# A hybrid decoder block: order of the first projections, of x's sums and of GLA's rstd product

## The chip, the cores and the metric

The kernel runs on one core of one Trainium2 chip. The metric is the device time of one execution in microseconds, the median of the runs shown; less is better.

## The reference, cut to what matters

One layer, batch 1, 256 tokens, model width 1024, all float32. `n = RMSNorm(x)` goes through one combined projection, whose columns are MoBA's q, k, v (512 each), GLA's q, k (512 each), GLA's v (1024), a rank-16 gate, an output gate (1024) and two branch gates (1024 each). MoBA (8 heads of 64) is causal attention with normed q and k and a T5 bias table; GLA (4 heads of 128) is a chunked gated linear attention. Both are mixed, projected, and a squared-ReLU feed-forward block follows.

```python
n = rms_norm(h, norm1_g[layer])
proj = n @ w_in[layer]
(mq, mk, mv, gq, gk, gv, g_low, g_out, gate_moba, gate_gla) = jnp.split(proj, IN_SPLIT_POINTS, axis=-1)
mq = rms_norm(mq.reshape(B, S, MOBA_HEADS, MOBA_HEAD_DIM), moba_q_norm_g[layer])
mk = rms_norm(mk.reshape(B, S, MOBA_HEADS, MOBA_HEAD_DIM), moba_k_norm_g[layer])
y_moba = moba_attention(mq, mk, mv, t5_bias)
log_a = log_sigmoid(g_low @ gla_gate_up + gla_gate_bias) / GLA_GATE_TAU
y_gla = gla_attention(gq, gk, gv, log_a)
h = h + (sigmoid(gate_moba) * (y_moba @ w_branch_moba) + sigmoid(gate_gla) * (norm(y_gla) * silu(g_out) @ w_branch_gla)) @ w_out
h = h + square(relu(rms_norm(h) @ w_up)) @ w_down
```

## The kernel before, in words

Every float32 product is made of three matmuls on parts: each operand is split into a rounded high part and the rest, and high x high, high x low and low x high are added in PSUM. The weights come in units of 1 MB (128 x 4 x 512). SyncE loads a unit (`load`, line 85), ScalarE copies it into the high part `wh` in two halves (`split`, line 94), and VectorE subtracts for the low part `wl` (`rest`, line 98). `rest` also asks for the load of the unit four places on.

The projection runs over `IN_ORDER`: MQ, MK, GQ, GK, MV, GV0, GV1 and so on, two units for each name (`hu` 0 to 25), and each unit in two turns t, one for each 128 tokens, or for GQ and GK one for each 128 columns. A turn is called a slot here: slot = 2 * hu + t. In slot s TensorE gets the unit's matmuls; then `flush` issues what the slot before deferred (its `rest`, and the VectorE part of its evictions); then `split` prepares a half of the unit two places on; then come the eviction of a finished accumulator and the steps that were hung on this slot with `at(slot, ...)`. MQ is slots 0 to 3, MK slots 4 to 7; before the change GQ is slots 8 to 11, GK 12 to 15, MV 16 to 19. Each engine takes its own instructions strictly in this order, so a late one holds all behind it.

Because x goes into the projection without its norm, each eviction multiplies by rstd. `x_stats` (line 237) sums x squared on ScalarE, VectorE and GpSimd make rstd from it (`rsqrt`, lines 218 and 219). MQ and MK are evicted by `m_evac` (lines 301 and 303 on ScalarE, then a reduction, line 308, and a `rsqrt` for each head), at slots 5 to 8 behind the other steps; `m_norm` (316) scales, `m_transpose` (324, then 287 and 288) turns q and k into high and low parts, and `m_scores0` (334) multiplies them, `m_scores1` follows. GQ and GK come out transposed, so their rstd lies along the free axis: `g_diag` and `g_row` (468 to 479) spread it into the row `rrow`, and `g_evac` adds two halves (542 on ScalarE, 545 on VectorE) and multiplies by that row (546 on VectorE). The GLA gate is `g_low` and `g_decay` (488 to 509), in which ScalarE and VectorE take turns on a bank (508, 509).

The T5 bias is made on the chip: `make_bias` (270, 272) puts a small table into DRAM as `ud`, `spread_bias` copies it to 128 rows `ur`, and `load_bias` reads it with a skew into `bias`, which line 345 of `m_scores0` adds. All three DMAs are issued by SyncE, in its queue between the weight loads. SyncE also loads, in this order at the start: x and the MQ weights, units 2 and 3, `vec`, x again for the sums (`xs`), the bias inputs, the gate weights, units 4 and 5.

Of the kernel before, what the change touches and what calls it, by code (L numbers as in the profile page):

```python
# [15 lines left out]
AF = mybir.ActivationFunctionType  # L16
OP = mybir.AluOpType
AX = mybir.AxisListType

S = 256  # L20
D = 1024
NT = 2
H = 8
DH = 64
GH = 4
DK = 128
# [9 lines left out]
MQ, MK, MV, GQ, GK, GV0, GV1 = 0, 512, 1024, 1536, 2048, 2560, 3072  # L36
GLOW = 3584
GO0, GO1, GA0, GA1, GG0, GG1 = 3600, 4112, 4624, 5136, 5648, 6160
TRANSPOSED = (GQ, GK)
IN_ORDER = (MQ, MK, GQ, GK, MV, GV0, GV1, GO0, GO1, GA0, GG0, GA1, GG1)  # L40


V_G2, V_GB, V_OG, V_QG, V_KG, NVEC = 0, 8, 12, 14, 15, 16
# [3 lines left out]
def block_kernel(ctx, tc, xw0_d, xw_d, x_d, vec_d, w_d, up_d, bias_d, out_d):  # L47
    nc = tc.nc
    P = 128
# [11 lines left out]
    def big(name, dt=F32):  # L61
        return t4.tile([P, 1024], dt, name=name, tag="t4")

    def mid(name):
        return t2.tile([P, 512], F32, name=name, tag="t2")
# [7 lines left out]
    def axbank(name):  # L73
        return ps.tile([P, 512], F32, name=name, tag="ax")
# [4 lines left out]
    def load(i, pieces=1):  # L79
        if i >= NHU:  # L80
            return
        raw[i] = wp.tile([P, 4, 512], F32, name=f"raw{i}", tag="raw", bufs=4)
        n = 4 // pieces
        for a in range(0, 4, n):
            nc.sync.dma_start(raw[i][:, a:a + n, :], w_d[i - 2, :, a:a + n, :])

    def split(i, a, n=2):
        if i >= NHU:
            return
        if a == 0:  # L90
            wH[i] = wp.tile([P, 4, 512], F32R, name=f"wh{i}", tag="wh")
            wL[i] = wp.tile([P, 4, 512], F32R, name=f"wl{i}", tag="wl")
        s = slice(a, a + n)
        nc.scalar.activation(wH[i][:, s, :], raw[i][:, s, :], AF.Copy)  # L94
        defer(rest, i, s)
# [10 lines left out]
    def defer(f, *a):  # L106
        deferred.append((f, a))

    def flush():
        now, deferred[:] = list(deferred), []  # L110
        for f, a in now:
            f(*a)
# [26 lines left out]
    vec = const.tile([P, NVEC + 128], F32, name="vec")  # L139
# [10 lines left out]
        nc.sync.dma_start(xw[kt], xw_d[kt - 1])  # L150
    load(2, 2)
    load(3)
    nc.sync.dma_start(vec, vec_d)

    NBR = bias_d.shape[0]
    smallR, smallS = big("smallR"), big("smallS", F32R)
# [66 lines left out]
    xs = [big(f"xs{t}") for t in range(NT)]  # L223
    for t in range(NT):
        nc.sync.dma_start(xs[t], x_d[:, t, :])
    nc.sync.dma_start(biasR, bias_d)
    nc.sync.dma_start(gup, up_d)
    load(4)
    load(5)

    rstd = const.tile([P, NT], F32, name="rstd")
# [14 lines left out]
    T = {}  # L246
# [15 lines left out]
    bias = t4.tile([P, H, 256], F32, name="bias", tag="t8", bufs=3)  # L262
# [5 lines left out]
    def make_bias():  # L268
        pb = axbank("pbias")
        nc.tensor.matmul(pb[:H, :384], biasS[:, :H], biasS[:, H:], start=True, stop=True)  # L270
        u = mid("u")[:H, :384]
        nc.vector.tensor_copy(u, pb[:H, :384])
        T["ud"] = dr.tile([H, 384], F32, name="ud")
        nc.sync.dma_start(T["ud"], u)

    def spread_bias():

        T["ur"] = dr.tile([P, H, 384], F32, name="ur")
        nc.sync.dma_start(T["ur"], T["ud"][None].to_broadcast([P, H, 384]))

    def load_bias():
        ur = T["ur"]
        nc.sync.dma_start(bias, bass.AP(tensor=ur.tensor, offset=ur.offset + 127,
                                        ap=[[H * 384 - 1, P], [384, H], [1, 256]]))

    def split_evac(dH, dL, src, scale):
# [5 lines left out]
    def m_evac(which, t, acc):  # L292
        if which == "mv":
            if t == 0:
                T["mvH"], T["mvL"] = (big(f"mv{a}", F32R).rearrange("p (t c) -> p t c", t=2) for a in "HL")
            split_evac(T["mvH"][:, t, :], T["mvL"][:, t, :], acc, rstd[:, t:t + 1])
            return
        if t == 0:
            T[which] = big(which)
        dst = T[which].rearrange("p (t c) -> p t c", t=2)[:, t, :]  # L300
        nc.scalar.activation(dst, acc, AF.Copy, scale=rstd[:, t:t + 1])
        sq = mid("sq")
        nc.scalar.activation(sq, acc, AF.Square, scale=rstd[:, t:t + 1])
        r = T[which, "r", t] = small("rsm", H)

        def finish():
            ss = small("ssm", H)
            nc.vector.tensor_reduce(ss, sq.rearrange("p (h d) -> p h d", d=DH), axis=AX.X, op=OP.add)
            rsqrt(r, ss, DH)

        defer(finish)
# [160 lines left out]
    rrow = const.tile([P, S], F32, name="rrow")  # L472
# [63 lines left out]
    def g_evac(which, h, acc):  # L536

        if h == 0:
            T[which] = big(which)
        v = T[which][:, h * S:(h + 1) * S]  # L540
        half = mid("half")[:, :S]
        nc.scalar.activation(half, acc[:, S:], AF.Copy)

        def finish():
            nc.vector.tensor_tensor(v, acc[:, :S], half, op=OP.add)
            nc.vector.scalar_tensor_tensor(v, v, DK ** -0.5 if which == "gq" else 1.0, rrow,
                                           op0=OP.mult, op1=OP.mult)

        defer(finish)

# [103 lines left out]
    def gate_evac(which, n, t, acc):  # L654
        if t == 0:
            T[which, n] = big(f"{which}{n}").rearrange("p (t c) -> p t c", t=2)
        nc.scalar.activation(T[which, n][:, t, :], acc, AF.Sigmoid, scale=rstd[:, t:t + 1])

    def gv_evac(g, t, acc):
        if t == 0:  # L660
            for a in "HL":
                T["gv" + a, g] = big(f"gv{a}{g}", F32R).rearrange("p (t c) -> p t c", t=2)
        split_evac(T["gvH", g][:, t, :], T["gvL", g][:, t, :], acc, rstd[:, t:t + 1])

    evac = {
        MQ: lambda t, a: m_evac("mq", t, a), MK: lambda t, a: m_evac("mk", t, a),
        MV: lambda t, a: m_evac("mv", t, a),
        GQ: lambda t, a: g_evac("gq", t, a), GK: lambda t, a: g_evac("gk", t, a),
        GV0: lambda t, a: gv_evac(0, t, a), GV1: lambda t, a: gv_evac(1, t, a),
        GO0: lambda t, a: silu_evac(0, t, a), GO1: lambda t, a: silu_evac(1, t, a),  # L670
        GA0: lambda t, a: gate_evac("A", 0, t, a), GA1: lambda t, a: gate_evac("A", 1, t, a),
        GG0: lambda t, a: gate_evac("G", 0, t, a), GG1: lambda t, a: gate_evac("G", 1, t, a),
    }


    steps = {}

    def at(slot, f, *a):
        steps.setdefault(slot, []).append((f, a))

    at(5, split_bias)
    at(8, make_bias)
    at(4, x_stats)
    at(6, g_diag)
    at(7, low_split)
    at(8, g_row)
    at(9, gup_split)
    at(9, m_norm, "mq", 0)
    at(10, m_norm, "mq", 1)
    at(10, spread_bias)  # L690
    at(11, m_norm, "mk", 0)
    at(11, g_low)
    at(12, m_norm, "mk", 1)
    at(13, m_transpose, "mq", 0)
    at(13, m_transpose, "mq", 1)
    at(14, g_decay, 0)
    at(14, g_decay, 1)
    at(14, load_bias)
    at(15, m_transpose, "mk", 0)
    at(15, m_transpose, "mk", 1)  # L700
    at(16, m_scores0)
    at(16, m_max, 0)
    at(17, m_softmax, 0, 0, 4)
    at(18, m_softmax, 0, 4, 8)
    at(19, m_scores1, 0)
    at(19, m_max, 1)
    at(19, m_weights, 0)
    at(20, m_softmax, 1, 0, 2)
    at(21, m_softmax, 1, 2, 4)
    at(22, m_scores1, 1)  # L710
    at(22, m_max, 2)
    at(22, m_weights, 1)
    at(23, m_softmax, 2, 0, 2)
    at(24, m_softmax, 2, 2, 4)
    at(25, g_logsig)
    at(26, g_scan)
    at(26, m_weights, 2)
    at(27, g_exp, "eb")
    at(28, g_exp, "einv")
    at(29, g_exp, "edec")  # L720
# [24 lines left out]
    at(50, g_yT, 1, 1)  # L745


    hu = 0
    for u, col in enumerate(IN_ORDER):
        acc = [] if col in TRANSPOSED else [(axbank if u == 1 else mmbank)(f"acc{t}") for t in range(NT)]  # L750
        for g in range(2):
            if u == 0:
                for k in range(4):
                    first_block(4 * g + k, acc)
            for t in range(NT):
                if col in TRANSPOSED:
                    acc = mmbank("acct")
                    for k in range(2):
                        block_t(hu, t, k, xHL[k], acc)
                elif u:  # L760
                    block(hu, t, xH[g], xL[g], acc[t], g == 0, g == 1)
                flush()
                split(hu + 2, 2 * t)
                if g == 1 and u < 2:
                    at(5 + 2 * u + t, evac[col], t, acc[t])
                elif col in TRANSPOSED:
                    evac[col](2 * g + t, acc)
                elif g == 1:
                    evac[col](t, acc[t])
                for f, a in steps.pop(2 * hu + t, []):  # L770
                    f(*a)
            hu += 1
    assert not steps


    mxH = [kview(big(f"mxH{g}", F32R)) for g in range(2)]
# [58 lines left out]
    for n in range(2):  # L835
        acc = [mmbank(f"po{t}") for t in range(NT)]
# [77 lines left out]
    acc = [axbank(f"pu{j}") for j in range(4)]  # L914
# [15 lines left out]
    for c in range(1, NC):  # L930
        for b in range(2):
            for j in range(2):
                acc = axbank(f"pu{j}")
# [86 lines left out]
```

## Time and profile before

| what | us |
|---|---|
| median of 3 runs (lowest to highest) | 424.98 (424.61 to 425.13) |
| the profiled execution, its own time | 424.48 |
| its span, first to last instruction | 422.8 |
| TensorE busy | 412.9 (98%) |
| VectorE busy | 285.9 (68%) |
| ScalarE busy | 222.5 (53%) |
| GpSimd busy | 17.8 (4%) |

The profile shows one execution. A busy share is an average over the whole span; a timeline row gives start and length of one instruction, and in brackets how long its engine was idle just before it and what ended that. The end of a matmul is modelled, and neighbours overlap in the rows, so TensorE's pace is read from one start to the next.

### The profile page before, as it was taken

To read this page: it belongs to the slowest core of one execution; us is meant where nothing else is said; L and a number is where in the kernel's file an instruction comes from. 1 tells how busy PE (TensorE), PEld (TensorE's weight loads), DVE (VectorE), ACT (ScalarE), POOL (GpSimd) and SP (SyncE) were. 2 spreads that over 40 slices of the span, in tenths; PEclk is the share of its full clock that TensorE was granted. 3 is DMA by queue.
4 is the path that set the end of the run, shared out by engine and by line. 5 is a ranking of instruction groups with operands and counts; after the bars stand their busy time and mean duration, and the time that the engine had idled before them with its cause. 6 is when DMAs were issued, how large, how long until landed. Compare 5 with 4: busy or idle time off the path is not lost.

```text
span 422.8 us, 5266 instructions
## 1 busy us (share of the span) xinstructions
PE 412.9 (98%) x2072; PEld 345.5 (82%) x2072; DVE 285.9 (68%) x374; ACT 222.5 (53%) x344; POOL 17.8 (4%) x21
## 2 busy tenths in 40 slices
PE   8999979999999999999999999999999999999996
PEld 5877957888888888888888888888888888888885
DVE  5838987688798543874856878848393848474753
ACT  5669562869865464553423446646362726263520
POOL 2006100000002011000000000000000000000000
PEclk9999996999999999999999999999999999999999
DMA  8995783245544252372675445645455463627002
GB/s 281 381 372 203 258 289 122 87 189 200 198 164 156 86 194 99 135 279 84 219 279 188 136 174 198 228 172 212 186 184 214 147 250 112 287 101 298 0 2 99
DMA packets 13848, 78.91 MB, mean 187 GB/s; under 512 B 1448, under 2 KB 3104, under 8 KB 5376
## 3 DMA queue, kind: packets, MB, share of 16 engines
q1 hardware_dynamic: 13392, 77.28, 50.0%
q10 hardware_dynamic: 432, 1.31, 0.9%
q8 instruction: 16, 0.26, 0.2%
q14 instruction: 8, 0.07, 0.0%
HBM read 77.52 MB, written 2.63 MB: 190 GB/s over the span
## 4 chain that ended last, share of the span: by engine, by line
PE 84%; DMA 5%; DVE 5%; ACT 4%; issue 1%; SPq 0%; ACTq 0%
PE pu L131 14%; PE acc L118 8%; PE acc L119 8%; PE acc L120 8%; PE pu L133 7%; PE fa L119 7%; PE fa L120 7%; PE fa L118 7%; DMA raw<-w 4%; PE po L118 2%; PE po L120 2%; PE pg L118 2%; PE po L119 2%; PE pg L120 2%; PE pg L119 2%; DVE wl L98 2%
## 5 line engine op out<-in xcount | busy, mean ns | idle before, releaser
L98 DVE TENSOR_TENSOR wl<-raw,wh 128x1024 fp32r<-128x1024 f32 x132 | 158.2, 1220 | 18.9 <-ACT wh L94 18.7
L94 ACT ACTIVATE wh<-raw 128x1024 fp32r<-128x1024 f32 x132 | 135.2, 1051 | 24.4 <-PE pg L120 9.8
L131 PE MATMUL pu<-hHL,wh 128*128 128x512 f32 x256 | 69.9, 394 | 0.0
L118 PE MATMUL acc<-wh,xHL 128*128 128x512 f32 x160 | 64.6, 404 | 0.0
L119 PE MATMUL acc<-wl,xHL 128*128 128x512 f32 x160 | 63.0, 394 | 0.0
L120 PE MATMUL acc<-wh,xHL 128*128 128x512 f32 x160 | 62.9, 393 | 0.0
L131 PEld LDWEIGHTS pu<-hHL,wh 128*128 128x128 f32 x256 | 44.3, 189 | 6.3
L120 PE MATMUL fa<-wh,fL 128*128 128x512 f32 x124 | 48.4, 390 | 0.0
L119 PE MATMUL fa<-wl,fH 128*128 128x512 f32 x124 | 48.4, 390 | 0.0
L118 PE MATMUL fa<-wh,fH 128*128 128x512 f32 x124 | 48.3, 389 | 0.0
L133 PEld LDWEIGHTS pu<-hHL,wl 128*128 128x128 f32 x256 | 39.3, 189 | 5.4
L133 PE MATMUL pu<-hHL,wl 128*128 128x256 f32 x256 | 40.7, 281 | 0.0
L870 ACT ACTIVATE half<-pu 128x256 f32<-128x256 f32 x32 | 12.0, 377 | 54.4 <-PE pu L133 54.4
L871 DVE TENSOR_TENSOR sq<-pu,half 128x256 f32<-128x256 f32 x32 | 13.5, 423 | 34.9 <-ACT half L870 34.2
L120 PEld LDWEIGHTS acc<-wh,xHL 128*128 128x128 f32 x160 | 30.4, 190 | 6.7
L118 PEld LDWEIGHTS acc<-wh,xHL 128*128 128x128 f32 x160 | 30.5, 190 | 6.3
L119 PEld LDWEIGHTS acc<-wl,xHL 128*128 128x128 f32 x160 | 30.6, 191 | 5.7
L120 PEld LDWEIGHTS fa<-wh,fL 128*128 128x128 f32 x124 | 23.3, 188 | 4.9
L118 PEld LDWEIGHTS fa<-wh,fH 128*128 128x128 f32 x124 | 23.3, 188 | 4.7
L119 PEld LDWEIGHTS fa<-wl,fH 128*128 128x128 f32 x124 | 23.3, 188 | 4.7
L876 ACT ACTIVATE fH<-sq 128x512 fp32r<-128x512 f32 x16 | 10.1, 632 | 20.6 <-DVE sq L873 20.6
L131 PE MATMUL acct<-xHL,wh 128*128 128x512 f32 x64 | 17.6, 396 | 0.0
(232 smaller groups left out, 533.8 us busy)
## 6 DMA issues: line engine op xcount, KB each, us to landing
raw<-w SPq DMA_DIRECT2D x65, 1024.0 KB, 4.8
xw<-xw SPq DMA_DIRECT2D x7, 384.0 KB, 6.5
ur<-ud SPq DMA_DIRECT2D x1, 1536.0 KB, 9.2
raw<-w SPq DMA_DIRECT2D x2, 512.0 KB, 7.3
xs<-xs SPq DMA_DIRECT2D x2, 512.0 KB, 8.7
bias<-ur SPq DMA_DIRECT2D x1, 1024.0 KB, 7.4
xr<-xs ACTq DMA_DIRECT2D x2, 512.0 KB, 4.8
out<-o SPq DMA_DIRECT2D x3, 256.0 KB, 2.0
```

The source lines that it names most:

```text
L94: nc.scalar.activation(wH[i][:, s, :], raw[i][:, s, :], AF.Copy)
L98: nc.vector.tensor_tensor(wL[i][:, s, :], raw[i][:, s, :], wH[i][:, s, :].bitcast(F32), op=OP.subtract)
L118: nc.tensor.matmul(acc, aH[:, k, tk], h, start=start and k == 0, stop=False)
L119: nc.tensor.matmul(acc, aH[:, k, tk], low, start=False, stop=False)
L120: nc.tensor.matmul(acc, aL[:, k, tk], h, start=False, stop=stop and k == 3)
L131: nc.tensor.matmul(acc, tile_(wH, k), a[:, k, :], start=g == 0 and k == 0, stop=False)
L133: nc.tensor.matmul(acc[:, :S], tile_(wL, k), a[:, k, :S], start=False, stop=g == 1 and k == 3)
L870: nc.scalar.activation(half, acc[:, S:], AF.Copy)
L871: nc.vector.tensor_tensor(o, acc[:, :S], half, op=OP.add)
L876: nc.scalar.activation(H, v, AF.Copy)
```

## The change

It moves MV from the fifth place of the projection to the third, so that MV is slots 8 to 11, GQ 12 to 15 and GK 16 to 19. The sums of x go to slot 3 (from 4); MQ's evictions go to slots 4 and 5 (from 5 and 6), MK's stay in slots 7 and 8, and all four are issued ahead of the slot's `split`. Unit 4's load is issued ahead of `vec` and the bias and gate inputs. The three DMAs of the bias are issued by GpSimd, the last at slot 12 (from 14). MoBA's scores, softmax and weights move one slot later each, up to `m_weights` 2, which goes from 26 to 27. In `g_evac` the add takes the scale along in one VectorE instruction, and the product with `rrow` is GpSimd's.

```diff
-IN_ORDER = (MQ, MK, GQ, GK, MV, GV0, GV1, GO0, GO1, GA0, GG0, GA1, GG1)
+IN_ORDER = (MQ, MK, MV, GQ, GK, GV0, GV1, GO0, GO1, GA0, GG0, GA1, GG1)
...
     load(3)
-    nc.sync.dma_start(vec, vec_d)
...
         nc.sync.dma_start(xs[t], x_d[:, t, :])
+    load(4)
+    nc.sync.dma_start(vec, vec_d)
     nc.sync.dma_start(biasR, bias_d)
     nc.sync.dma_start(gup, up_d)
-    load(4)
     load(5)
...
-        nc.sync.dma_start(T["ud"], u)
+        nc.gpsimd.dma_start(T["ud"], u)
...
-        nc.sync.dma_start(T["ur"], T["ud"][None].to_broadcast([P, H, 384]))
+        nc.gpsimd.dma_start(T["ur"], T["ud"][None].to_broadcast([P, H, 384]))
...
-        nc.sync.dma_start(bias, bass.AP(tensor=ur.tensor, offset=ur.offset + 127,
+        nc.gpsimd.dma_start(bias, bass.AP(tensor=ur.tensor, offset=ur.offset + 127,
...
-        nc.scalar.activation(half, acc[:, S:], AF.Copy)
+        scale = DK ** -0.5 if which == "gq" else 1.0
+        nc.scalar.activation(half, acc[:, S:], AF.Copy, scale=scale)
         def finish():
-            nc.vector.tensor_tensor(v, acc[:, :S], half, op=OP.add)
-            nc.vector.scalar_tensor_tensor(v, v, DK ** -0.5 if which == "gq" else 1.0, rrow,
-                                           op0=OP.mult, op1=OP.mult)
+            nc.vector.scalar_tensor_tensor(v, acc[:, :S], scale, half, op0=OP.mult, op1=OP.add)
+            nc.gpsimd.tensor_tensor(v, v, rrow, op=OP.mult)
...
-    at(5, split_bias)
-    at(8, make_bias)
-    at(4, x_stats)
+    at(3, x_stats)
     at(6, g_diag)
-    at(7, low_split)
     at(8, g_row)
+    at(7, split_bias)
+    at(8, low_split)
     at(9, gup_split)
+    at(9, make_bias)
...
+    at(12, load_bias)
...
-    at(14, load_bias)
...
-    at(16, m_scores0)
-    at(16, m_max, 0)
-    at(17, m_softmax, 0, 0, 4)
+    at(17, m_scores0)
+    at(17, m_max, 0)
+    at(18, m_softmax, 0, 0, 4)
...
-    at(26, m_weights, 2)
+    at(27, m_weights, 2)
...
                 flush()
+                for f, a in early.pop(2 * hu + t, []):
+                    f(*a)
                 split(hu + 2, 2 * t)
                 if g == 1 and u < 2:
-                    at(5 + 2 * u + t, evac[col], t, acc[t])
+                    early.setdefault(4 + 3 * u + t, []).append((evac[col], (t, acc[t])))
```

## Rows read from the trace of the kernel before

**Rows 1.** Waits of TensorE: waiter, releaser, total us, times, longest.

```profile
PE ps L334 <- DVE mkL L288: 2.9, 1, 2.9
```

**Rows 2.** Busy time of each engine by stretch, with granted clock and DMA share.

```profile
27.75:33.38 5.63, 4.19 (x21) 2.82 (x20) 3.42 (x9) 5.07 (x10) 2.20 (x2) 1.00 0.77 292
33.38:57.45 24.07, 24.04 (x149) 21.18 (x149) 22.61 (x41) 15.55 (x30) 6.91 (x4) 1.00 0.70 245
57.45:67.15 9.70, 6.08 (x40) 4.98 (x38) 6.58 (x12) 5.54 (x9) 0.00 (x0) 0.82 0.81 287
67.15:77.98 10.83, 10.83 (x49) 8.60 (x48) 6.64 (x7) 6.24 (x20) 0.00 (x0) 0.85 0.28 98
```

**Rows 3.** Timeline of TensorE, 27 to 37 us: start, length, line, operation.

```profile
27.75 1.07 PE L131 MATMUL acct<-xHL,wh 128*128 128x512 f32 x4
...
31.06 0.74 PE L133 MATMUL acct<-xHL,wl 128*128 128x256 f32 x4 [0.64 <-DVE wl L98]
...
32.69 0.85 PE L478 MATMUL prow<-diag,ones 128*128 128x256 f32 x2 [0.72 <-ACT diag L469]
33.38 1.09 PE L131 MATMUL acct<-xHL,wh 128*128 128x512 f32 x4
...
36.18 1.08 PE L131 MATMUL acct<-xHL,wh 128*128 128x512 f32 x4
```

**Rows 4.** Timeline of TensorE and its weight loads, 56 to 68 us.

```profile
56.38 0.42 PEld L324 LDWEIGHTS pt<-ident,mk 128*128 128x128 f32 x4 [0.23 <-DVE mqL L288]
...
60.06 0.39 PE L120 MATMUL acc<-wh,xHL 128*128 128x512 f32 x1
...
64.39 0.47 PE L334 MATMUL ps<-mkL,mqH 64*128 64x128 f32 x1 [2.92 <-DVE mkL L288]
...
67.15 0.79 PE L118 MATMUL acc<-wh,xHL 128*128 128x512 f32 x1
```

**Rows 5.** Timeline of ScalarE, 25 to 31 us.

```profile
25.06 1.06 ACT L94 ACTIVATE wh<-raw 128x1024 fp32r<-128x1024 f32 x1 [5.50 <-DMA raw<-w]
...
28.02 0.19 ACT L237 ACTIVATION_READ_ACCUMULATOR junk<-xs 128x1 f32 x1
...
29.48 0.67 ACT L301 ACTIVATE mq<-acc,rstd 128x512 f32<-128x512 f32 x1
...
30.61 1.05 ACT L94 ACTIVATE wh<-raw 128x1024 fp32r<-128x1024 f32 x1
```

**Rows 6.** Groups of VectorE instructions by shape, 26 to 66 us: busy us, mean ns.

```profile
L546 DVE SCALAR_TENSOR_TENSOR gq<-gq,rrow 128x256 f32<-128x256 f32 x4 | 1.7, 425 | 0.6 <-ACT wh L94 0.5
...
L288 DVE SCALAR_TENSOR_TENSOR mkL<-pt,vec,mkH 128x512 fp32r<-128x512 f32 x2 | 1.4, 742 | 0.0
```

**Rows 7.** Instructions of line 98, whole span: shortest, median, longest ns.

```profile
L98 DVE TENSOR_TENSOR wl<-raw,wh x132: 1202/1219/1226, 14.8 to 411.8; 128x1024 fp32r<-128x1024 f32 x132
```

**Rows 8.** Timeline of VectorE, 37 to 69 us.

```profile
37.66 0.54 DVE L272 COPY u<-pbias 8x384 f32<-8x384 f32 x1
...
63.60 1.40 DVE L288 SCALAR_TENSOR_TENSOR mkL<-pt,vec,mkH 128x512 fp32r<-128x512 f32 x2
67.03 1.29 DVE L345 SCALAR_TENSOR_TENSOR s<-ps,bias 128x512 f32<-128x512 f32 x2 [2.04 <-PE ps L334]
```

**Rows 9.** Timeline of GpSimd, 120 to 135 us.

```profile
127.25 0.40 POOL L563 COPY gx<-eb 128x256 f32<-128x256 f32 x1 [83.64 <-PE py L425]
129.43 1.33 POOL L568 COPY gx<-edec 128x256 f32<-128x256 f32 x1 [1.79 <-DVE edec L553]
```

**Rows 10.** Issues by SyncE: one timeline row; then KB each, us to landing.

```profile
11.60 0.43 SPq L225 DMA_DIRECT2D xs<-xs  x1
...
xs<-xs SPq DMA_DIRECT2D x1, 512.0 KB, 9.6
...
ur<-ud SPq DMA_DIRECT2D x1, 1536.0 KB, 9.2
...
bias<-ur SPq DMA_DIRECT2D x1, 1024.0 KB, 7.4
```

More of the change, by code (lines that the diff above doesn't have):

```diff
@@ L697, in block_kernel @@
     at(14, g_decay, 1)
-    at(14, load_bias)
     at(15, m_transpose, "mk", 0)
     at(15, m_transpose, "mk", 1)
-    at(16, m_scores0)
-    at(16, m_max, 0)
-    at(17, m_softmax, 0, 0, 4)
[L704 to L714, printed above, removed]
+    at(17, m_scores0)
+    at(17, m_max, 0)
+    at(18, m_softmax, 0, 0, 4)
+    at(19, m_softmax, 0, 4, 8)
+    at(20, m_scores1, 0)
+    at(20, m_max, 1)
+    at(20, m_weights, 0)
+    at(21, m_softmax, 1, 0, 2)
+    at(22, m_softmax, 1, 2, 4)
+    at(23, m_scores1, 1)
+    at(23, m_max, 2)
+    at(23, m_weights, 1)
+    at(24, m_softmax, 2, 0, 2)
+    at(25, m_softmax, 2, 2, 4)
     at(25, g_logsig)
     at(26, g_scan)
-    at(26, m_weights, 2)
+    at(27, m_weights, 2)
     at(27, g_exp, "eb")
@@ L745, in block_kernel @@
     at(50, g_yT, 1, 1)
-    hu = 0
+    hu, early = 0, {}
     for u, col in enumerate(IN_ORDER):
@@ L772, in block_kernel @@
             hu += 1
-    assert not steps
+    assert not steps and not early
     mxH = [kview(big(f"mxH{g}", F32R)) for g in range(2)]
```

## Prediction, made before the change was run

> **What bounds the kernel now.** I read the page's busy times first: TensorE is busy 98% of the span, so only its few gaps and its slow stretches can be won. The second view is the list of TensorE's waits. It names six, none later than 64.39 us; the longest is the first scores' wait for the low part of MoBA's k [rows 1]. The third is the busy time by stretch [rows 2]: between 27.75 and 77.98 us there are two places where TensorE loses time, and a granted clock below 1.00 around the second. The fourth is TensorE's timeline at these two places.
>
> *First place, unit 4* [rows 3]. Slots there repeat every 36.18 - 33.38 = 2.80 us; I use this for all slots. A slot is 4 x 512 and 4 x 256 columns, twice, so 512 columns take 0.23 us. From 27.75 to 33.38 TensorE ran slot 8, the bias table (384 columns) and the rstd row (2 x 256), at that pace 2.80 + 0.40 us. It took 5.63: **2.43 us are lost**, waiting for unit 4's low part and then for the diagonal of rstd, of whose two parts the second is late too. The cause is on ScalarE [rows 5]. It stood idle 5.50 us until unit 4's weights landed at 25.06; the sums of x, though x's second half had landed at 11.60 + 9.6 = 21.2 us [rows 10], are queued behind that split and end at 28.2; MQ's first eviction starts at 29.48.
>
> *Second place, the first scores* [rows 4]. The last matmul of slot 16 starts at 60.06, so the scores could start at 60.29. They go on in earnest at 64.39, when VectorE has the low part of k, and the next unit starts at 67.15. VectorE is the late one: busy 22.61 of the 24.07 us before 57.45 [rows 2], it reaches that low part at 63.60 [rows 8], and it works without a break behind work that piled up at the first place. After some 4 us without much work the clock falls to its lower level (1.2 GHz): 0.18 x 2 x 9.70 = 3.5 us of it before 67.15 and 0.15 x 2 x 10.83 = 3.25 us behind [rows 2]. The loss of 2.43 us at the first place, in two pieces, left it at 1.00. The scores themselves took 2.76 us at half clock, so 1.38 at full. Lost here: 67.15 - 60.29 - 1.38 = **5.48 us**, and half of the later 3.25, **1.6 us**.
>
> Between them the transposes of k wait 0.23 us for a bank that VectorE still reads [rows 4]; their second half waits as long again: **0.47 us**. After 78 us TensorE is never kept waiting.
>
> **The change part by part.** *Sums and evictions first.* The sums take 2 x 1.05 us; the second can't start before 21.2 and ends by 22.2. From the end of the sums to the first MQ eviction it took 29.48 - 28.21 = 1.27 us [rows 5], so that is at 23.5. A pair of evictions takes 30.61 - 29.48 = 1.13, a split pitches at 0.95 (1.05 with the overlap), the subtraction takes 1.22 [rows 7]: first eviction to 24.6, half of unit 4 to 25.55, second eviction to 26.7, second half to 27.65, its low part to 28.9. TensorE starts unit 4 at 27.75 and asks for this low part after seven of twelve matmuls, at 29.35. Margin 0.45 us. Unit 4's weights come at 25.06 at the latest; as its load passes three small ones, rather sooner. At 25.06 the margin is nil. The diagonal follows on VectorE behind 28.9 and takes about 1.2 us with its two hand-overs; the row is due at 27.75 + 2.80 = 30.55. Margin 0.4. So I count the 2.43 us as won, with up to 1 us back in the range. What follows on ScalarE starts earlier by what went into its idle time, the sums and one eviction, 2.1 + 1.1 us, less the wait for unit 5's weights: I take 2.7 and bound it by 0 and 3.3.
>
> *MV third.* The same units run, so TensorE's work is the same. What changes is what VectorE must have done before the low part of k. GQ's four products of 0.425 us leave VectorE [rows 6], GK's four products and four sums, of the same shape (8 x 0.42), come behind the scores, together -5.1 us; MV's two low parts come ahead, of the shape of k's, which take 1.40 for two [rows 6, 8]: +1.4. Net -3.7. Before, VectorE ended k's low part at 63.60 + 1.40 = 65.0; after, at 65.0 - 3.7 - 2.7 = 58.6. The scores, one slot later, are due at 60.29 + 2.80 - 2.43 - 0.47 = 60.2. Margin 1.6 us. So the 5.48, the 0.47 and the 1.6 us go, and with the wait the fall of the clock.
>
> *GpSimd's product.* The trace has no product of this shape on GpSimd. Its copies of 128x256 took 0.40 and 1.33 us [rows 9]; with two inputs I take 0.7, and 0.40 to 1.33 as bounds. One comes per slot of 2.80 us, and nobody reads GQ or GK before slot 31, so on GpSimd it costs nothing. GpSimd's queue has the head norms' roots ahead of the first DMA, so none waits behind one; the products behind `load_bias` wait for `ur`, harmlessly. PSUM is freed by VectorE's sum, not by the product. The scale folded into the sum costs nothing (0.42 either way).
>
> *The bias.* SyncE's queue loses three DMAs, which saves TensorE nothing, as no load waits there long enough to be late. GpSimd's queue gains them. The table's copy was at 37.66 [rows 8]; it is a slot later in order on an engine 2.7 us earlier, so about 38.5. No DMA by GpSimd is in the trace. At SyncE's prices, 9.2 and 7.4 us [rows 10] and something between 0 and 7.4 (I take 3) for the first, the bias lands at 58; bounds 55 and 62.5, and 86.5 if each takes twice as long. The scores want it at 60.2 + 1.38 = 61.6. Late, it first delays only VectorE: behind the sum with the bias (1.3 us), the maximum and one subtraction (1.2 each) and GK's second sum stands the bank that slot 21 needs, at 61.6 + 3 x 2.80 + 0.9 = 70.9. So a landing up to about 66.9 costs TensorE nothing.
>
> *One slot less for the softmax.* VectorE and ScalarE have 2.8 us less between scores and the GLA steps; before, VectorE still idled 2.04 us for the first scores [rows 8], and nothing later made TensorE wait. I take 0, with 2.8 as the upper bound.
>
> **Sum.** 2.43 + 0.47 + 5.48 + 1.6 = 10.0 us. The profiled execution took 424.48 us (422.8 of span and 1.7 around it) and would take 414.5; the median of the runs is 0.5 above it, so the forecast is **415.0**.
>
> **The rivals.** *The read port.* VectorE's line 98 reads two operands from SBUF, as does GpSimd's product. The first copy on GpSimd took 0.40 us; the second, issued just as a line 98 began, took 1.33 [rows 9]: GpSimd seems to wait for VectorE. The reverse is not in the trace: 132 instructions of line 98 lie within 1202 to 1226 ns [rows 7], but GpSimd read hardly anything beside them. Two such subtractions stand in the last 5 us ahead of k's low part. If each is held up by 0.40 to 1.33 us, k is 0.8 to 2.7 us later, 0 to 1.1 beyond the margin: 415.0 to 416.1. If all four GQ products, let loose together when `ur` lands, hold VectorE 1.33 us each, it is 5.3 - 1.6 = 3.7 us late, and with the half clock (3.4) the time is 422. The Trainium skill (SBUF — State Buffer, Who interferes with whom) speaks for this and against the change: a VectorE instruction with two SBUF inputs and a GpSimd one that reads SBUF exclude each other, and whichever started first blocks the other for all its length. By that rule VectorE would give back up to the 3.4 us that it saves with eight products; the trace agrees with it in one direction only.
>
> *The sums don't get ahead.* If x lands later, or the evictions hold ScalarE while unit 4 waits, the first loss stays, whole or in part: 415.0 + 2.4 = 417.4. Against it stands the landing at 21.2, for it the margin of 0.45.
>
> *Slower: the bias through GpSimd.* If its DMAs take twice SyncE's 9.2 and 7.4, the bias lands near 38.5 + 3 + 18.4 + 14.8 = 74.7, 7.8 us behind the point of 66.9 from which it decides; with the half clock 415.0 + 7.8 + 3.4 = 426.2, and 438 at the bound of 86.5. Against it: the engines that carry the data are shared, and they had room (DMA share 0.28 behind 67 us, 0.70 before 57) [rows 2].
>
> **How the numbers follow.** Forecast, within 414.0 to 416: 0.62. VectorE late by a little, or a wait of the softmax, 416 to 418.5: 0.12; late enough to bring the clock down, 419.8 to 424: 0.07. The first loss stays, 416 to 418.5: 0.12. Bias late: 0.07, of this 0.05 slower than 425.8 and 0.02 within 0.2% of before. A difference of 0.2%, 0.85 us, is about what a measurement here can tell from none. Range 414.0 to 419.8, holding a little over 0.8. Faster 0.93, same 0.02, slower 0.05.
>
> **What would show it.** Right: TensorE's timeline without a break from 10 to 110 us, clock 1.00 throughout, the sums of x ending near 22.2, MQ's first eviction near 23.5, k's low part done near 58.6 and the scores started near 60.2. Wrong: line 98 longer than 1.23 us beside a GpSimd product (the port); a wait of TensorE for unit 4 or the rstd row (the sums); the sum with the bias released by a DMA later than 67 us. If the clock falls anywhere, the forecast is off by 3 us or more.

## The result, and the profile after

The changed kernel takes **414.65 us** (414.03 to 414.74), the kernel before, run beside it, 424.8 (423.94 to 425.13): a ratio of 0.9761, interval 0.9743 to 0.9779, so 2.4% faster. The profiled execution took 414.74 us, its span is 413.0. The forecast was 415.0. One execution of all those told below, at 829.21 us, lies far from its fellows and is left out of its kernel's times.

The list of TensorE's waits in the kernel after, first; the wait for the low part of k [rows 1] is gone from it with all others but the one before the first instruction:

```profile
PE pwarm L167 <- PEq L1014: 0.8, 1, 0.8
```

The same stretches as [rows 2]: TensorE is busy for all of each one, and the granted clock is 1.00 in all four.

```profile
27.75:33.38 5.63, 5.63 (x28) 4.67 (x27) 3.57 (x9) 5.07 (x9) 2.02 (x1) 1.00 0.96 399
33.38:57.45 24.07, 24.07 (x144) 21.18 (x143) 21.94 (x36) 17.07 (x29) 10.10 (x8) 1.00 0.79 285
57.45:67.15 9.70, 9.70 (x71) 8.44 (x70) 8.15 (x12) 4.93 (x14) 3.02 (x4) 1.00 0.40 128
67.15:77.98 10.83, 10.83 (x58) 8.76 (x57) 8.67 (x11) 7.38 (x20) 1.84 (x3) 1.00 0.48 183
```

TensorE's timeline at the first place, which answers to [rows 3]: the rstd row follows the last matmul of slot 8 at the usual 0.23 us, and slot 9 follows it at once. The first row is the first matmul of slot 8, the last the first of slot 9.

```profile
27.83 0.39 PE L118 MATMUL acc<-wh,xHL 128*128 128x512 f32 x1
...
30.32 0.40 PE L120 MATMUL acc<-wh,xHL 128*128 128x512 f32 x1
30.56 0.40 PE L478 MATMUL prow<-diag,ones 128*128 128x256 f32 x2
30.80 0.40 PE L118 MATMUL acc<-wh,xHL 128*128 128x512 f32 x1
```

ScalarE there, for [rows 5]: the sums end at 21.67, ahead of unit 4's split, and MQ's first eviction follows.

```profile
21.48 0.19 ACT L237 ACTIVATION_READ_ACCUMULATOR junk<-xs 128x1 f32 x1
22.70 0.69 ACT L301 ACTIVATE mq<-acc,rstd 128x512 f32<-128x512 f32 x1 [1.03 <-POOL rstd L218]
...
23.85 1.06 ACT L94 ACTIVATE wh<-raw 128x1024 fp32r<-128x1024 f32 x1
```

The second place, for [rows 4]: the scores start at 60.23 right behind GK's unit and end by 61.72 at full clock, 1.5 us instead of 2.76.

```profile
59.67 0.63 PE L133 MATMUL acct<-xHL,wl 128*128 128x256 f32 x4
60.23 0.34 PE L334 MATMUL ps<-mkH,mqH 64*128 64x128 f32 x2
...
61.72 1.19 PE L131 MATMUL acct<-xHL,wh 128*128 128x512 f32 x4
```

VectorE, for [rows 8]: the low part of unit 4's second half is done at 28.28; k's low parts at 57.44 + 1.40 = 58.84; the sum with the bias waits for the scores, not for a DMA; one subtraction of line 98 took 1.55 us instead of 1.22.

```profile
27.05 1.23 DVE L98 TENSOR_TENSOR wl<-raw,wh 128x1024 fp32r<-128x1024 f32 x1
...
57.44 1.40 DVE L288 SCALAR_TENSOR_TENSOR mkL<-pt,vec,mkH 128x512 fp32r<-128x512 f32 x2
...
61.82 1.29 DVE L345 SCALAR_TENSOR_TENSOR s<-ps,bias 128x512 f32<-128x512 f32 x2 [1.51 <-PE ps L334]
...
67.79 1.55 DVE L98 TENSOR_TENSOR wl<-raw,wh 128x1024 fp32r<-128x1024 f32 x1 [0.50 <-ACT wh L94]
```

GpSimd: it issues the load of the bias at 50.42, behind the landing of `ur`, and the products behind it, two at once.

```profile
50.42 0.92 POOL L283 DMA_DIRECT2D bias<-ur  x1 [8.48 <-DMA ur<-ud]
51.36 1.44 POOL L547 TENSOR_TENSOR gq<-gq,rrow 128x256 f32<-128x256 f32 x2
56.13 2.36 POOL L547 TENSOR_TENSOR gq<-gq,rrow 128x256 f32<-128x256 f32 x2 [3.33 <-DVE gq L546]
```

### The profile page after: what moved, and what is told of

It reads as the page before. It is cut to its first block, busy times and chain, and to the rows that moved or that the text cites. A ratio compares the mean times of both kernels' runs of the same rounds, so it can differ in the third digit from the quotient of the medians.

```text
span 413.0 us, 5270 instructions
## 1 busy us (share of the span) xinstructions
PE 408.9 (99%) x2072; PEld 343.3 (83%) x2072; DVE 283.1 (69%) x366; ACT 223.0 (54%) x344; POOL 29.2 (7%) x32
## 3 DMA queue, kind: packets, MB, share of 16 engines
q1 hardware_dynamic: 12192, 74.64, 49.4%
## 4 chain that ended last, share of the span: by engine, by line
PE 97%; DMA 1%; ACT 0%; SPq 0%; DVE 0%; issue 0%
PE pu L131 14%; PE acc L118 9%; PE acc L119 9%; PE acc L120 9%; PE pu L133 7%; PE fa L119 7%; PE fa L120 7%; PE fa L118 7%; PE acct L131 4%; PE acct L133 2%; PE po L120 2%; PE po L118 2%; PE pg L118 2%; PE po L119 2%; PE pg L120 2%; PE pg L119 2%
## 5 line engine op out<-in xcount | busy, mean ns | idle before, releaser
L118 PE MATMUL acc<-wh,xHL 128*128 128x512 f32 x160 | 63.6, 398 | 0.0
L120 PE MATMUL acc<-wh,xHL 128*128 128x512 f32 x160 | 62.4, 390 | 0.0
```

The lines of the kernel that those rows point to most:

```text
L118: nc.tensor.matmul(acc, aH[:, k, tk], h, start=start and k == 0, stop=False)
L120: nc.tensor.matmul(acc, aL[:, k, tk], h, start=False, stop=stop and k == 3)
```

## Experiments: which part carried the gain

The theory: TensorE lost its time at two places, both because VectorE or ScalarE came late, and the parts of the change act only through the moment at which these have the two things that TensorE asks for. The rival for each part is that it earns or costs time by itself. The kernel before took 423.6 to 424.8 us in the four sets of runs; a saving is told against the median of its own set. The changed kernel itself was run in the first set alone, so a comparison with its 414.65 us crosses sets. The profiled executions differ before either place is reached: TensorE starts slot 8 at 27.83 in the changed kernel and at 26.69 in the one with MV back in fifth place, which starts alike. So "nothing" below means less than about 1 us, and the margins are read within one trace.

### The product with the rstd row back on VectorE

```diff
-            nc.gpsimd.tensor_tensor(v, v, rrow, op=OP.mult)
+            nc.vector.tensor_tensor(v, v, rrow, op=OP.mult)
```

> The changed kernel with the product with the rstd row given back to VectorE (after the add with the scale). My sum: four GQ products of 0.42 us stand ahead of the low part of MoBA's k, which in the changed kernel was done at 58.84 us for scores that started at 60.23; so it is done at about 60.5 and TensorE waits 0.3 us there: 414.6 to 415.2 us, no fall of the clock. Rival 'read port' (GpSimd's product takes as much from VectorE as it saves): k's low part is done no later than now, 414.0 to 414.6. Rival 'the product was what won the second place': late by 2 us or more with the clock down, 419 or more.

Measured: 414.48 us (414.04 to 415.02), ratio 0.9778 (0.9753 to 0.9802), clock 1.00, no wait for k's low part in the list. VectorE, then TensorE:

```profile
58.77 1.40 DVE L288 SCALAR_TENSOR_TENSOR mkL<-pt,vec,mkH 128x512 fp32r<-128x512 f32 x2
```

```profile
59.32 0.32 PE L334 MATMUL ps<-mkH,mqH 64*128 64x128 f32 x1
59.57 0.32 PE L334 MATMUL ps<-mkL,mqH 64*128 64x128 f32 x1
```

The first of the two low parts is done at 59.5 and the first scores read that one alone, so they run on at 59.57, about 0.1 us late. VectorE has come to the very edge of its margin, as the sum said, and the time is that of the changed kernel. GpSimd's product bought slack, and no time.

### The bias's DMAs back on SyncE

```diff
-        nc.gpsimd.dma_start(T["ud"], u)
+        nc.sync.dma_start(T["ud"], u)
...
-        nc.gpsimd.dma_start(T["ur"], T["ud"][None].to_broadcast([P, H, 384]))
+        nc.sync.dma_start(T["ur"], T["ud"][None].to_broadcast([P, H, 384]))
...
-        nc.gpsimd.dma_start(bias, bass.AP(tensor=ur.tensor, offset=ur.offset + 127,
+        nc.sync.dma_start(bias, bass.AP(tensor=ur.tensor, offset=ur.offset + 127,
```

> The changed kernel with the three DMAs of the bias back in SyncE's queue, in the new slots. My sum counts their move at nothing: 414.6, within 0.8 us either way; the bias lands between 55 and 63 us. Rival 'GpSimd's DMAs cost': 1 us or more faster. Rival 'GpSimd's queue was needed' (SyncE's weight loads held up behind the waits for the table, then late): 1 us or more slower, with a wait of ScalarE or TensorE for weights in the trace.

Measured: 414.59 us (414.49 to 414.9), ratio 0.9782 (0.9758 to 0.9806). The bias, issued at 49.4, landed 6.7 us later, at 56.1, ahead of the 58.8 by GpSimd's queue, but nobody asks for it before 61.7. The move is worth nothing either way.

### The old start

```diff
-    at(3, x_stats)
+    at(4, x_stats)
...
-                    early.setdefault(4 + 3 * u + t, []).append((evac[col], (t, acc[t])))
+                    at(5 + 2 * u + t, evac[col], t, acc[t])
```

(and `vec`, the bias inputs and the gate weights ahead of unit 4 again; `split_bias`, `low_split` and `make_bias` keep their new slots)

> The changed kernel with the start as it was: sums in slot 4, MQ's and MK's evictions behind the splits in slots 5 to 8, unit 4's load behind the small inputs. My sum: the first place loses its 2.43 us again (a wait for unit 4's low part near 30 us and one for the diagonal), 417.1 us; the scores are due 2.4 us later too and VectorE 2.7 us later, so they wait 0 to 0.5 us and the clock stays up: 416.8 to 417.8. Rival 'the start carries the second place too': VectorE's pile comes back, scores late by 2 us or more and the clock down, 420 to 422.

Measured: 416.53 us (416.31 to 417.41), ratio 0.9833 (0.98 to 0.9866), a little below the range that I gave, and 1.9 us above the changed kernel. TensorE waits at the first place again, and nowhere behind it; the clock stays at 1.00. The first row is the first matmul of slot 8, the last the first of slot 9: 4.71 us apart, where the changed kernel has 30.80 - 27.83 = 2.97, so 1.7 us are lost here, which is about what the time shows.

```profile
27.66 0.39 PE L118 MATMUL acc<-wh,xHL 128*128 128x512 f32 x1
...
29.84 0.50 PE L119 MATMUL acc<-wl,xHL 128*128 128x512 f32 x1 [0.43 <-DVE wl L98]
...
31.69 0.85 PE L478 MATMUL prow<-diag,ones 128*128 128x256 f32 x2 [0.42 <-ACT diag L469]
32.37 0.40 PE L118 MATMUL acc<-wh,xHL 128*128 128x512 f32 x1
```

### MV back in fifth place

```diff
-IN_ORDER = (MQ, MK, MV, GQ, GK, GV0, GV1, GO0, GO1, GA0, GG0, GA1, GG1)
+IN_ORDER = (MQ, MK, GQ, GK, MV, GV0, GV1, GO0, GO1, GA0, GG0, GA1, GG1)
```

> The changed kernel with MV back in fifth place, all else as changed, the scores still in slot 17. Counted by instruction: GK's four sums (4 x 0.42) come ahead of k's low part and MV's two low parts (1.4) behind it, so with the products on GpSimd k is only 0.3 us later than the 58.84 us of the changed kernel and the scores still don't wait: 414.4 to 415.2. Rival, as my prediction's sentence on MV third could be read (the new order wins the second place): k late by 2 us or more, 417 to 422.

Measured: 414.4 us (413.53 to 415.1), ratio 0.9774 (0.9748 to 0.9799). With the other parts in place, the order of the projection is worth no time. VectorE, then TensorE:

```profile
38.43 1.09 DVE L316 TENSOR_TENSOR mq<-mq,rsm 128x512 f32<-128x512 f32 x1
...
41.51 1.76 DVE L98 TENSOR_TENSOR wl<-raw,wh 128x1024 fp32r<-128x1024 f32 x1
...
47.58 1.76 DVE L98 TENSOR_TENSOR wl<-raw,wh 128x1024 fp32r<-128x1024 f32 x1
...
58.14 1.40 DVE L288 SCALAR_TENSOR_TENSOR mkL<-pt,vec,mkH 128x512 fp32r<-128x512 f32 x2
```

```profile
59.19 0.33 PE L334 MATMUL ps<-mkH,mqH 64*128 64x128 f32 x2
```

It is worth slack, and more than I had counted. The low part for the first scores is done at 58.14 + 0.74 = 58.88 for scores that start at 59.19: of the changed kernel's margin of 2.0 us (60.23 against 57.44 + 0.74) 0.3 are left, where I expected a loss of 0.3. Beside GpSimd's products two subtractions took 1.76 us instead of 1.22, and one product of line 316 1.09 instead of 0.69: 1.5 us that the count by instruction did not have.

### The scores back in slot 16

```diff
-    at(17, m_scores0)
+    at(16, m_scores0)
...
-    at(27, m_weights, 2)
+    at(26, m_weights, 2)
```

(with all of MoBA's steps between them one slot earlier)

> The changed kernel with MoBA's scores, softmax and weights back in their old slots (scores 16), all else as changed. The first scores read the low part of k for the first 128 tokens alone, which the changed kernel has at 57.44 + 0.75 = 58.2 us; in slot 16 they are due at 57.4: a wait of 0.8 us, no fall of the clock, 415.4 us (414.8 to 416.0). Rival 'the later slot wins the second place': a wait of 2 us or more with the clock down, 418 to 422.

Measured: 415.07 us (414.66 to 415.39), ratio 0.9784 (0.9751 to 0.9816), clock 1.00. TensorE waits, but briefly:

```profile
57.42 0.33 PE L334 MATMUL ps<-mkL,mqH 64*128 64x128 f32 x1 [0.33 <-DVE mkL L288]
```

So without the later slot the other parts leave a wait of 0.33 us by the list; beside them the later slot is mostly margin.

### The start alone

Only the start's part of the diff (loads, sums, evictions, and the slots of `split_bias`, `low_split` and `make_bias`), applied to the kernel before.

> The kernel before with the new start alone (sums in slot 3, first evictions ahead of the splits, unit 4's load first, the bias and low splits moved as in the change); order, scores, DMAs of the bias and products as before. The first place's 2 to 2.4 us go. VectorE has the low part of k about 2.7 us earlier, but it is due 2.9 us earlier: the scores still wait some 4 us and the clock still falls. 2.4 us faster than before (1.9 to 2.9). Rival 'the start carries the second place too': 6 us or more faster.

Measured: 421.62 us (420.95 to 421.87) beside 423.91 for the kernel before: 2.3 us, ratio 0.9936 (0.9912 to 0.996). The first two rows are the first matmuls of slots 8 and 9: 3.01 us apart, and 3.18 with the bias table (384 columns, 0.17 us), which now runs behind slot 9, against 5.63 before [rows 3]. So the first place is won whole, 2.4 us.

```profile
27.20 1.07 PE L131 MATMUL acct<-xHL,wh 128*128 128x512 f32 x4
...
30.21 1.09 PE L131 MATMUL acct<-xHL,wh 128*128 128x512 f32 x4
...
61.20 0.47 PE L334 MATMUL ps<-mkL,mqH 64*128 64x128 f32 x1 [2.92 <-DVE mkL L288]
```

The second place is as it was, 3.2 us earlier in the span (61.20 against 64.39 [rows 4]), clock and all; a wait and a stretch:

```profile
PE ps L334 <- DVE mkL L288: 2.9, 1, 2.9
```

```profile
57.45:67.15 9.70, 6.28 (x32) 5.34 (x33) 7.55 (x12) 3.65 (x8) 0.00 (x0) 0.68 0.46 160
```

VectorE comes earlier by as much as TensorE does: the start alone can't win the second place.

### MV third and the later slot, alone

The new `IN_ORDER` and MoBA's steps one slot later, applied to the kernel before.

> The kernel before with MV third and the scores one slot later, the start, the bias's DMAs and the products as before. The low part of k for the first 128 tokens comes at 64.35 - 3.4 (GK's eight instructions behind it) + 1.4 (MV's two ahead) = 62.4 us, due at 60.29 + 2.80 - 0.47 = 62.6: no wait, clock up: 7.0 to 7.6 us faster than before. Rival 'without the start and GpSimd VectorE stays late': 4 us faster or less, with the clock down.

Measured: 416.64 us (416.54 to 416.8) beside 423.91: 7.3 us, ratio 0.9818 (0.9792 to 0.9845). No wait for k's low part is left, the clock is 1.00, and what remains is the first place, now a wait of an ordinary unit:

```profile
PE acc L119 <- DVE wl L98: 1.1, 1, 1.1
```

### The later slot alone

MoBA's steps one slot later and nothing else, applied to the kernel before.

> The kernel before with the scores, softmax and weights one slot later and nothing else. The low part of k stays at 64.35 us, due at 62.6: a wait of 1.7 us. If the clock stays up (1.4 us of waiting left it up at the first place), 5.4 us faster than before; if it falls, 2.5 us faster. Rival 'the wait is VectorE's pile, a later slot only moves it': less than 1.5 us faster.

Measured: 419.65 us (419.24 to 420.1) beside 423.91: 4.3 us, ratio 0.9889 (0.986 to 0.9918), between the two cases that I had set. The wait is shorter than I had it, and yet the clock fell behind it:

```profile
PE ps L334 <- DVE mkL L288: 1.0, 1, 1.0
```

```profile
57.45:67.15 9.70, 8.73 (x51) 6.97 (x50) 9.11 (x14) 5.67 (x8) 0.00 (x0) 0.88 0.66 227
67.15:77.98 10.83, 10.83 (x53) 8.62 (x53) 7.41 (x10) 7.19 (x21) 0.00 (x0) 0.95 0.53 195
```

0.12 x 2 x 9.70 and 0.05 x 2 x 10.83 make 3.4 us at the lower level, so 1.7 us lost, beside the wait of 1.0. The new order without the later slot was not run on the kernel before; given the slot, it adds the 3.0 us between 4.3 and the 7.3 of the experiment before.

### MV fifth and the product on VectorE, together

The edits of the first and the fourth experiment in one kernel.

> The changed kernel with MV back in fifth place and the product with the rstd row back on VectorE; start, later slot and the bias's DMAs as changed. Each alone cost nothing, as the low part of k still came in time. Together k's low part has eight products of 0.42 us more ahead of it than with the old order alone: 1.1 to 2 us late, so TensorE waits that long and the clock falls for part of the time, as with the later slot alone: 416 to 418. Rival 'neither matters': 414.2 to 415.2.

Measured: 416.2, 417.07 and 417.7 us, ratio 0.9838 (0.9793 to 0.9883). Each of the two edits alone cost nothing, both together bring the wait back:

```profile
PE ps L334 <- DVE mkL L288: 1.0, 1, 1.0
```

In its profiled execution (416.2 us) the clock did not fall: the same two stretches as above have

```profile
57.45:67.15 9.70, 8.73 (x55) 7.04 (x54) 9.60 (x14) 5.24 (x9) 0.00 (x0) 1.00 0.48 176
67.15:77.98 10.83, 10.83 (x57) 8.68 (x56) 8.85 (x11) 8.41 (x25) 0.00 (x0) 1.00 0.57 194
```

The order and the product are substitutes: either keeps VectorE in time, if barely, and without both it is late.

### Both of GpSimd's parts taken back

The edits of the first two experiments in one kernel: nothing new is left on GpSimd.

> The changed kernel with both of GpSimd's parts taken back: the product with the rstd row on VectorE and the three DMAs of the bias on SyncE. Each alone cost nothing; k's low part for the first scores comes about as they are due (within 0.1 us in the kernel with the product alone taken back). So 414.2 to 415.2. Rival 'they cover for each other' (together they make VectorE or the loads late): 416 or more.

Measured: 414.71 us (414.35 to 415.32), ratio 0.9777 (0.975 to 0.9804), clock 1.00, no wait at either place. The start, the order and the later slot make the whole gain, and the two halves add up: 2.3 us for the start alone and 7.3 for order and slot alone are 9.6; this kernel is 9.6 us faster than the kernel before beside it.

### Long products on GpSimd

```diff
+    def g_spin():
+        nc.gpsimd.tensor_tensor(smallR, seg, seg, op=OP.mult)
...
+    for n in (13, 14, 15, 16):
+        at(n, g_spin)
```

> The changed kernel with four more GpSimd products of 128x1024 out of SBUF, one in each of slots 13 to 16, behind GQ's products and into a tile that nobody reads. At four times the columns of the 0.74 us product I expect about 2.7 us each. Theory 'whoever starts first holds the other': subtractions of line 98 that come while such a product runs last up to 1.2 + 2.7 us, more than the one of 1.55 us in the changed kernel; the two ahead of k's low part lose 0.5 to 3 us together, against a margin of 2.0: 414.4 to 416. Rival 'only GpSimd waits' (as the trace of before showed it): line 98 stays within 1.23 us, the long products are stretched, 414.2 to 415.0.

Measured: 414.63 us (414.14 to 416.43), ratio 0.9781 (0.9746 to 0.9816). The long products took 1.9 us each, not 2.7. VectorE, then GpSimd:

```profile
53.76 3.12 DVE L98 TENSOR_TENSOR wl<-raw,wh 128x1024 fp32r<-128x1024 f32 x1
```

```profile
53.21 0.73 POOL L550 TENSOR_TENSOR gq<-gq,rrow 128x256 f32<-128x256 f32 x1
53.90 1.89 POOL L475 TENSOR_TENSOR smallR<-seg 128x1024 f32<-128x1024 f32 x1
```

The subtraction that began beside GpSimd's product took 3.12 us instead of 1.22: it ended 1.09 us behind the end of the second product (53.90 + 1.89 = 55.79), which is about its own length, so it seems to have done nothing until then. That settles the direction that the trace of before left open: GpSimd does hold VectorE. The other traces agree. The longest line 98 lasts 1.4 to 3.1 us in all seven kernels that have the product on GpSimd, and at most 1.23 us in all seven that have it on VectorE; shortest, median and longest, of the changed kernel and of the one with the product back on VectorE:

```profile
L98 DVE TENSOR_TENSOR wl<-raw,wh x132: 1198/1219/1551, 14.8 to 402.2; 128x1024 fp32r<-128x1024 f32 x132
L98 DVE TENSOR_TENSOR wl<-raw,wh x132: 1201/1219/1227, 13.9 to 401.6; 128x1024 fp32r<-128x1024 f32 x132
```

The 1.9 us stayed within the margin at k's low part, and the time is unchanged.

### The bias made late

```diff
     def load_bias():
-        ur = T["ur"]
+        ur = T["ur2"] = dr.tile([P, H, 384], F32, name="ur2")
+        nc.gpsimd.dma_start(ur, T["ur"])
```

> The changed kernel with one more copy of the spread bias table in DRAM, on GpSimd's queue, ahead of the load of the bias: its price as the spread itself, 8.8 us. The bias then lands at about 59.8 + 9 = 68.5 to 69 us instead of 59.8, for a sum that wants it at 61.6. My prediction puts the point from which TensorE pays at 66.9: so VectorE waits some 7 us, TensorE 1.5 to 2.5 us for the bank of slot 21, 416 to 417.5 with the clock up, 419 with it down. Rival 'any lateness of the bias is paid': 7 us or more slower, 421 and up. Rival 'the bias isn't waited for': 414.6.

Measured: 416.32 to 419.43 us, median 417.66, ratio 0.9847 (0.9806 to 0.9888). VectorE waits 7.6 us for the bias, TensorE 2.7 us; VectorE's rows, then TensorE's:

```profile
67.84 1.29 DVE L346 SCALAR_TENSOR_TENSOR s<-ps,bias 128x512 f32<-128x512 f32 x2 [7.64 <-DMA bias<-ur]
69.16 1.22 DVE L371 TENSOR_REDUCE nmax<-s 128x8 f32<-128x1024 f32 x1
70.30 1.22 DVE L98 TENSOR_TENSOR wl<-raw,wh 128x1024 fp32r<-128x1024 f32 x1
```

```profile
68.49 0.39 PE L118 MATMUL acc<-wh,xHL 128*128 128x512 f32 x1
71.57 0.79 PE L119 MATMUL acc<-wl,xHL 128*128 128x512 f32 x1 [2.69 <-DVE wl L98]
```

The bias was issued at 60.09 and landed 7.6 us later, at 67.7. The four executions fall in two pairs: 416.32 and 416.46 us with a mean clock of 1.00, 418.87 (the profiled one) and 419.43 with 0.995 and 0.992. Most of the lateness is absorbed, as predicted, but TensorE pays at another place than I had named: it asks for the low part of unit 10's second half, which stands on VectorE right behind the maximum.

## Why the prediction was right, point by point

**The two places and the sum.** I summed 2.43 + 0.47 + 5.48 + 1.6 = 10.0 us; the medians differ by 10.15, the profiled executions by 424.48 - 414.74 = 9.74. Nothing that I had counted as won came back later. By the experiments the first place is worth 1.9 (old start) to 2.3 us (start alone; 2.4 in its trace), against 2.43, and the second 7.3 us (order and slot alone), against 7.55.

**The start.** The sums ended at 21.67 (22.2 predicted), MQ's first eviction started at 22.70 (23.5), the low part of unit 4 was there at 28.28 (28.9), with 1.1 us of margin. The steps are right, each somewhat early.

**k's low part.** I had both halves done at 58.6 and the scores due at 60.2; they were done at 58.84, and the scores started at 60.23. One term was mis-sized on the safe side: the first scores are those of the first 128 tokens and read the first half alone, 0.7 us earlier, so the margin was 2.0 us and not 1.6. The kernel with the product back on VectorE lived on just that.

**What wins the second place.** My heading "MV third" counted -3.7 us of VectorE's work and put GpSimd's four products for GQ among them. The sum holds for all parts together. As a statement on the order alone it would be wrong: with the other parts in place the old order costs nothing (414.4), nor does the product on VectorE (414.48), while both together bring the wait back (416.2 to 417.7). What TensorE sees is only whether VectorE is in time; several parts buy the same thing. There is not much more of it than is needed: with the old order 0.3 us of margin is left, with the product on VectorE none.

**GpSimd's product.** I took 0.7 us and counted it at nothing. It takes 0.73 us free, and about 1.65 where it meets a line 98. The rival of the read port was right as a mechanism, and my sign for it, a line 98 longer than 1.23 us, did appear: 1.55 us in the changed kernel, 3.12 with the long products. It cost no time because both stayed within VectorE's slack. With the old order it took 1.5 us, most of the margin; so it stayed without a price by the margin, which I had not sized for it. The rule of the Trainium skill (SBUF — State Buffer, Who interferes with whom) holds in both directions in these rows; that it would cost VectorE as much as eight products save does not.

**The bias.** I had it land at 58, with GpSimd's DMAs at SyncE's prices. The profile lists 8.8 us for the spread and 8.4 for the load, issued at 50.42, so it landed at 58.8, ahead of the 61.8 at which it was wanted. The step that failed is the point from which lateness is paid. I put it at 66.9, by the bank of slot 21. The late bias landed at 67.7 and cost 2.7 us of waiting, so the point lies near 65.1: unit 10's second half is split in slot 17, its low part is deferred to slot 18, behind the sum with the bias, and TensorE asks for it in the middle of slot 20. I had looked for the next bank and overlooked the nearer subtraction. The slower rival thus decided 1.8 us earlier than I wrote; it still was 6 us away.

**The softmax's missing slot** cost nothing, as taken.

## What to carry to other kernels

Where TensorE is busy all the time but for a few places, find which engine is late at each place, and count its queue from the last moment when it was idle to the thing that is asked for; work that is taken out of that queue, moved behind, or done in an idle time ahead of it all buy the same slack, and once the slack is there, more of it buys nothing. Test the parts alone and in pairs: here five single edits taken back cost 0 to 1.9 us, which would make a gain of 10 us look as if it came from nowhere. When asking from when a late thing is paid, list all that stands behind it on its engine, and take the earliest thing that TensorE wants, not the most conspicuous.

## What the hardware showed that was not expected

*The clock can fall behind a wait of 1 us.* In the kernel with the later slot alone the list gives TensorE 1.0 us of waiting, then scores that use half the array, and the granted clock fell to 1.2 GHz for 3.4 us. In the kernel with order and product undone the same wait of 1.0 us ahead of the same scores left it at 1.00, and so did the wait of 1.1 us at the first place of the kernel with order and slot. At the first place of the kernel before, two waits of 0.64 and 0.72 us left it at 1.00 too [rows 3]. What decides is not settled by these runs. Some of the scatter of these kernels goes with the clock, as in the two pairs of the late bias. Not all of it does: with the later slot alone the slowest of four executions, 420.1 us, is the only one with a mean clock of 1.00; the other three, at 0.994 and 0.995, took 419.24 to 419.94.

*A VectorE instruction that waits for GpSimd may be overtaken.* With the long products, the subtraction stood ready from 53.76; GpSimd's product of that moment ended at 53.94, and yet the next one of GpSimd, started at 53.90, went first. So the subtraction paid for two GpSimd instructions in a row, 1.9 us in all. It is one case, and GpSimd's starts are rough in the profile. In the same trace another subtraction got through between two of them: it stood ready from 59.91, was done at 61.88, 1.08 us behind the end of the product that held it (60.80), and GpSimd's next one, started at 60.76, took 1.72 us instead of 0.73. VectorE, then GpSimd:

```profile
59.91 1.97 DVE L98 TENSOR_TENSOR wl<-raw,wh 128x1024 fp32r<-128x1024 f32 x1
```

```profile
58.91 1.89 POOL L475 TENSOR_TENSOR smallR<-seg 128x1024 f32<-128x1024 f32 x1
60.76 1.72 POOL L550 TENSOR_TENSOR gq<-gq,rrow 128x256 f32<-128x256 f32 x1
```
